# A block inversion done in place, beside a scan: fewer VectorE steps, an input copied in two parts, other PSUM banks

## The chip, the cores and the metric

The kernel runs on one core of a Trainium2 chip. The metric is device time in microseconds (us), median over runs. A core has TensorE (PE, with its weight loads shown apart as PEld), VectorE (DVE), ScalarE (ACT), GpSimd (POOL) and SyncE (SP, which issues DMAs); each takes its instructions in order. All data is float32; products that need full precision are made of three products of split operands (a high and a low part).

## The reference, cut to what matters

The model is a two-layer trunk: a spatial-gating layer, a gated ConvFFN, an RWKV-7 layer, a second ConvFFN, and a final norm, for 512 tokens of width 1024. The change lies in the RWKV-7 layer, 16 heads of width 64:

```python
kk = heads(k * k_k)
kk = kk * lax.rsqrt(jnp.maximum(jnp.sum(kk * kk, -1, keepdims=True), 1e-24))
k = k * (1 + (a - 1) * k_a)
...
y = wkv7_scan(r_h, decay, k_h, v_h, -kk, kk * a_h)

def step(state, inp):
    r_t, w_t, k_t, v_t, a_t, b_t = inp
    sa = jnp.einsum('bhvk,bhk->bhv', state, a_t)
    state = (state * w_t[:, :, None, :]
             + sa[..., None] * b_t[:, :, None, :]
             + v_t[..., None] * k_t[:, :, None, :])
    y_t = jnp.einsum('bhvk,bhk->bhv', state, r_t)
    return state, y_t
```

The kernel does this scan in chunks of 64 tokens. Within a chunk the recurrence is a triangular system, so every chunk of every head needs the inverse of a 64x64 unit triangular matrix: 8 chunks x 16 heads.

## The kernel before, in words

Tokens lie along the free axis, features along the 128 partitions: a tile is 128 features by 512 tokens, and two heads make a "pair" of 128 features. There are 8 pairs in two groups g of four. `rwkv_main` runs these generators:

- `pairs()`, per pair p: `decay` (decays and the norm of kk), `operands`, `products`. In `decay` the sum of squares of kk per head is four products of `sq` with `blk2` (two columns, one per head, L920); DVE turns the 8 columns into reciprocals (L922, L923), and PE spreads them (L928). In `products`, chunk products land in the PSUM banks "aux" (one head) and "us" (the other) (L970), are masked by DVE (L974), and ACT copies the triangular part into `ti[g]` (L975); a second set (L984) uses the same banks.
- `invert(g)`: the inverse of the 32 matrices (4 pairs x 8 chunks) per head half of group g, as 32x32 diagonal blocks on DVE and off-diagonal blocks on PE. The blocks are copied to `x` (L1035 DVE for g = 1, L1037 ACT for g = 0), transposed to `li` (L1040), and `tt` is set to the identity by POOL (L1031, L1032). A loop over j = 0 to 30 multiplies a column with a row of `li` into `pr` (L1050) and adds it to `tt` (L1051). Two transposes make `z` and `y` (L1040). Then come PE's off-diagonal products (L1069, L1072) into "aux" banks, with ACT's copies out (L1082, L1084) and of the diagonal blocks (L1077).
- `scan(g)`: the chunk recurrence of a group, a chain of small products (L1275, L1279, L1288, L1295, L1300) with DVE, ACT and POOL steps between them (L1278, L1289, L1290, L1299, L1284, L1303), and `finish`.
- `fill`: projections, gates and the output projection, whose long products keep PE busy beside the rest (L325 to L327, in `mm3`).

Every bank name has two buffers. `weave` puts the generators together: at each `yield` of the main one it takes so many steps of a side generator and of `fill`, with rates written out by hand (`RATES`). A planner then orders each engine's instructions by its own costs, so the order on an engine can differ from that of the program. The first inversion runs beside the last pairs; the second starts when the first makes its off-diagonal products, and its loop runs on beside `scan(0)`.

Of the kernel before, what the change touches and what calls it, by code (L numbers as in the profile page):

```python
# [12 lines left out]
F32 = mybir.dt.float32  # L13
F32R = mybir.dt.float32r
AF = mybir.ActivationFunctionType
ALU = mybir.AluOpType
# [4 lines left out]
P = 128  # L21
D = 1024
KT = 8
T = 512
NF = 22
C = 64
# [118 lines left out]
class Emit:  # L145
# [622 lines left out]
    def rwkv_main(self, r, ctx, gain):  # L768
        nc, tc, A = self.nc, self.tc, self.A
        V, S, G = nc.vector, nc.scalar, nc.gpsimd  # L770
# [5 lines left out]
        ip = r.ip  # L776
        ep = ctx.enter_context(tc.tile_pool(name="pairs", bufs=1))

        def tile_(shape, tag, bufs):
            return ep.tile(shape, F32, tag=tag, bufs=bufs, name=self.uid(tag))  # L780

        def tmp(tag, bufs, w=W2):
            return tile_([P, w], tag, bufs)

        def c3(t):
            return t.rearrange("p (c t) -> p c t", t=C)
# [9 lines left out]
        def second_factors(p):  # L796

            w32 = self.l2w.pop()
            l2[:] = [ep.tile([P, 2 * P], F32R, tag=f"l2{i}", bufs=1, name=self.uid("l2")) for i in range(3)]
            for j in range(2):  # L800
                w = w32[:, 512 * j:512 * j + 2 * P]
                S.copy(l2[j], w)
                V.tensor_tensor(l2[2][H[j]], w[H[j]], l2[j][H[j]].bitcast(F32), ALU.subtract)
            if p + 2 < KT:
                self.load_l2(p + 2)
# [82 lines left out]
        def scratch(tag):  # L888
            return self.gp.tile([P, T], F32, tag=tag, bufs=2 if tag == "sq" else 1, name=self.uid(tag))

        def decay(p, u):

            k, w = ks[p], slice(p % 2 * P, (p % 2 + 1) * P)
            accs = [self.acc("e") for _ in range(2)]
            for j in range(2):
                nc.tensor.matmul(accs[j], l2[j][:, w], r.lr[j], start=True, stop=False)
            for j in range(2):
                nc.tensor.matmul(accs[j], l2[2][H[j], w], r.lr[j][H[j]], start=False, stop=True)
            if p % 2 == 1 and p + 1 < KT:
                second_factors(p + 1)  # L900
            th, u.ta = scratch("sq"), tmp("ta", 2, T)
            for j, x in enumerate((th, u.ta)):
                S.activation(x, accs[j], AF.Tanh, scale=0.5, bias=dq(j, p))
            u.kn = tmp("kn", 2, T)
            S.activation(u.kn, k, AF.Copy, scale=dq(2, p))
            V.tensor_scalar(th, th, 1.0, None, ALU.add)
            yield
            V.tensor_tensor_scan(th, self.c("smask", T), th, 0.0, ALU.mult, ALU.add)
            sq = scratch("sq")
            S.activation(sq, u.kn, AF.Square)  # L910
            u.gt = tile_([P, NCH, C + 1], "gt", 1)
            G.memset(u.gt[:, :, 0:1], 1.0)
            S.activation(u.gt[:, :, 1:], c3(th), AF.Exp, scale=C1)
            S.activation(gc[:, p], c3(th)[:, :, C - 1], AF.Exp, scale=C1)
            u.ei = scratch("rb")
            S.activation(u.ei, th, AF.Exp, scale=-C1)

            q = self.acc("e")
            for b in range(4):
                nc.tensor.matmul(q[:, 2 * b:2 * b + 2], sq[:, b * P:(b + 1) * P], self.c("blk2", 2), start=True, stop=True)  # L920
            n2 = tile_([P, 8], "n2", 2)
            V.tensor_scalar(n2, q[:, 0:8], 1e-24, None, ALU.max)  # L922
            V.reciprocal(n2, n2)  # L923
            yield
            u.q = self.acc("e")
            for b in range(4):
                for hd in range(2):
                    nc.tensor.matmul(u.q[H[hd], b * P:(b + 1) * P], n2[:, 2 * b + hd:2 * b + hd + 1].to_broadcast([P, C]),  # L928
                                     self.c("ident", P), start=True, stop=True)
            yield  # L930
# [87 lines left out]
        def invert(g):  # L1018

            tg = ti[g].rearrange("p i c t -> p (i c) t")
            Q = [(slice(64 * hd + 32 * b, 64 * hd + 32 * b + 32), slice(32 * b, 32 * b + 32))
                 for hd in range(2) for b in range(2)]

            def blocks(tag):
                return ip.tile([P, 32, 32], F32, tag=tag, bufs=2, name=self.uid(tag))

            x, li, tt = blocks("ix"), blocks("li"), blocks("tt")
            pr = ip.tile([P, 272], F32, tag="pr", bufs=1, name=self.uid("pr"))  # L1030
            G.memset(tt, 0.0)  # L1031
            G.memset(tt.rearrange("p s t -> p (s t)")[:, 0:1024:33], 1.0)  # L1032
            for n, (rows, cols) in enumerate(Q):
                if g == 1:
                    V.tensor_copy(x[rows], tg[rows, :, cols])  # L1035
                else:
                    S.copy(x[rows], tg[rows, :, cols])  # L1037
            def turn(out, src):
                for bs in [slice(n, n + 8) for n in range(0, 32, 8)] if g == 1 else [slice(0, 32)]:
                    V.transpose(out[:, bs], src[:, bs])  # L1040

            turn(li.rearrange("p s t -> p t s"), x.rearrange("p u t -> p t u"))
            for _ in range(WAIT):
                yield
            for j in range(31):
                ni, nj = 31 - j, j + 1
                a = li[:, j, j + 1:32].unsqueeze(1).to_broadcast([P, nj, ni])
                b = tt[:, 0:nj, j].unsqueeze(2).to_broadcast([P, nj, ni])
                q = pr[:, 0:ni * nj].rearrange("p (c i) -> p c i", i=ni)
                V.tensor_tensor(q, a, b, ALU.mult)  # L1050
                V.tensor_tensor(tt[:, 0:nj, j + 1:32], tt[:, 0:nj, j + 1:32], q, ALU.add)  # L1051
                if j % 2 == 1:
                    yield

            z, y = blocks("ix"), blocks("li")
            turn(z.rearrange("p u t -> p t u"), tt)
            turn(y.rearrange("p u t -> p t u"), tt.rearrange("p s t -> p t s"))
            yield
            off, own = blocks("tt"), iter(Q)
            for i in range(2):  # L1060
                for hf in range(2):
                    ps = self.acc("aux").rearrange("p (u t) -> p u t", t=32)
                    us = slice(16 * hf, 16 * hf + 16)
                    for u in range(16):
                        for hd in range(2):
                            b0, b1 = Q[2 * hd][0], Q[2 * hd + 1][0]
                            n = 16 * hf + u
                            if i == 0:
                                nc.tensor.matmul(ps[b1, u, :], tg[b0, n, 32:64], z[b0, n, :], start=True, stop=True,  # L1069
                                                 tile_position=(b0.start, b1.start))  # L1070
                            else:
                                nc.tensor.matmul(ps[b0, u, :], off[b1, n, :], y[b1, n, :], start=True, stop=True,  # L1072
                                                 tile_position=(b1.start, b0.start))
                        if u % 8 == 7:
                            if i == 0:
                                rows, cols = next(own)
                                S.copy(tg[rows, :, cols], y[rows])  # L1077
                            yield
                    for hd in range(2):
                        b0, b1 = Q[2 * hd][0], Q[2 * hd + 1][0]  # L1080
                        if i == 0:
                            S.copy(off[b1, us], ps[b1])  # L1082
                        else:
                            S.copy(tg[b0, us, 32:64], ps[b0])  # L1084
# [287 lines left out]
        def until(gen, end):  # L1372
            for _ in gen:
                yield
                if end():
                    return


        fill = itertools.chain(projections(), gates(), project())
        gw, ga = {}, {}  # L1380
        main = pairs()
        self.weave(until(main, lambda: 3 in done), None, fill, *RATES[0], ktiles=STEPS[0])
        inv = invert(0)
        for _ in take(inv, FIRST0):
            pass
        self.weave(until(main, lambda: KT - 2 in done), inv, fill, *RATES[1], ktiles=STEPS[1])
        load(0, 0)
        self.weave(main, inv, fill, *RATES[5], ktiles=STEPS[1])
        ahead = invert(1)
        for _ in inv:  # L1390
            next(fill)
            self.step(ahead, (mybir.EngineType.PE,))
# [83 lines left out]
```

## Time and profile before

| | |
|---|---|
| median of 3 runs | 1255.08 us (1254.97 to 1259.6) |
| profiled execution, its own time | 1255.64 us |
| its span, first to last instruction | 1253.5 us |
| PE busy | 1235.4 us (99%) |
| PEld, DVE, ACT, POOL busy | 80%, 68%, 50%, 7% |
| mean granted PE clock | 0.997 |
| RWKV pairs and inversions, scans | about 570 to 730 us, 728 to 856 us |

Times below are of the profiled execution, counted from its span's start. A row of a stretch gives, after its length, busy time and instruction count of each engine, the granted PE clock as a share of full speed, the DMA engines' busy share, and GB/s. A row of a group ends in busy time, mean ns of one, and idle time just before. In a row of the timeline the bracket tells how long the engine stood idle before, and who ended that.

### The profile page before, as it was taken

To read this page: it belongs to the slowest core of one execution; us is meant where nothing else is said; L and a number is where in the kernel's file an instruction comes from. 1 tells how busy PE (TensorE), PEld (TensorE's weight loads), DVE (VectorE), ACT (ScalarE), POOL (GpSimd) and SP (SyncE) were. 2 spreads that over 40 slices of the span, in tenths; PEclk is the share of its full clock that TensorE was granted. 3 is DMA by queue.
4 is the path that set the end of the run, shared out by engine and by line. 5 is a ranking of instruction groups with operands and counts; after the bars stand their busy time and mean duration, and the time that the engine had idled before them with its cause. 6 is when DMAs were issued, how large, how long until landed. Compare 5 with 4: busy or idle time off the path is not lost.

```text
span 1253.5 us, 19402 instructions
## 1 busy us (share of the span) xinstructions
PE 1235.4 (99%) x7535; PEld 1002.0 (80%) x7535; DVE 857.8 (68%) x1416; ACT 628.2 (50%) x1081; POOL 83.4 (7%) x110
## 2 busy tenths in 40 slices
PE   8999999999999999999999999899999999999997
PEld 6878888888888888877777777677888888888886
DVE  5566568888886454775789898675677777772323
ACT  6544455555554333475676657433544445442322
POOL 1100200000000010000000023222100000000000
PEclk9999999999999999999999999999999999999999
DMA  7332457777656776326878797644322333233332
GB/s 269 96 106 81 134 175 244 243 250 244 202 166 205 222 219 183 108 86 189 219 199 227 220 281 215 215 152 135 101 94 92 101 101 96 91 95 97 106 93 80
DMA packets 125132, 201.65 MB, mean 161 GB/s; under 512 B 39856, under 2 KB 63152, under 8 KB 125040
## 3 DMA queue, kind: packets, MB, share of 16 engines
q10 hardware_dynamic: 38976, 112.87, 29.6%
q1 hardware_dynamic: 86064, 87.54, 22.6%
q8 instruction: 59, 0.97, 0.3%
q14 instruction: 33, 0.27, 0.1%
HBM read 152.93 MB, written 47.45 MB: 160 GB/s over the span
## 4 chain that ended last, share of the span: by engine, by line
PE 90%; DVE 5%; DMA 2%; ACT 1%; issue 1%; POOL 0%; SPq 0%; POOLq 0%; DVEq 0%; ACTq 0%
PE mm L325 9%; PE mm L326 9%; PE mm L327 9%; PE aux L325 6%; PE aux L327 6%; PE aux L326 6%; PE e L325 6%; PE e L326 6%; PE us L325 6%; PE e L327 6%; PE us L327 6%; PE us L326 6%; PE aux L970 1%; DVE tt L1051 1%; DVE pr L1050 1%; PE aux L984 1%
## 5 line engine op out<-in xcount | busy, mean ns | idle before, releaser
L237 ACT CAST w<-w 128x512 fp32r<-128x512 f32 x340 | 205.9, 611 | 350.5 <-PE aux L327 89.1
L238 DVE TENSOR_TENSOR w<-w,w 128x512 fp32r<-128x512 f32 x340 | 231.1, 682 | 181.6 <-ACT w L237 181.2
L325 PE MATMUL mm<-mxh,w 128*128 128x512 f32 x408 | 166.7, 409 | 0.0
L326 PE MATMUL mm<-mxl,w 128*128 128x512 f32 x408 | 160.9, 394 | 0.9 <-DVE mxl L1188 0.9
L327 PE MATMUL mm<-mxh,w 128*128 128x512 f32 x408 | 160.3, 393 | 0.0
L325 PEld LDWEIGHTS mm<-mxh,w 128*128 128x128 f32 x408 | 76.8, 188 | 19.6 <-issue 3.3
L326 PEld LDWEIGHTS mm<-mxl,w 128*128 128x128 f32 x408 | 76.8, 188 | 16.5 <-issue 1.3
L327 PEld LDWEIGHTS mm<-mxh,w 128*128 128x128 f32 x408 | 76.7, 188 | 16.6 <-issue 0.7
L575 ACT ACTIVATE cv<-z,par 128x512 f32<-128x512 f32 x88 | 71.7, 816 | 32.5 <-DVE z L573 27.6
L325 PE MATMUL aux<-mxh,w 128*128 128x512 f32 x216 | 84.5, 391 | 0.0
L325 PE MATMUL us<-mxh,w 128*128 128x512 f32 x216 | 84.5, 391 | 0.0
L327 PE MATMUL aux<-mxh,w 128*128 128x512 f32 x216 | 84.2, 390 | 0.0
L326 PE MATMUL aux<-mxl,w 128*128 128x512 f32 x216 | 84.1, 389 | 0.0
L326 PE MATMUL us<-mxl,w 128*128 128x512 f32 x216 | 84.1, 389 | 0.0
L327 PE MATMUL us<-mxh,w 128*128 128x512 f32 x216 | 84.1, 389 | 0.0
L354 POOL TENSOR_TENSOR ss<-ss,sq 128x512 f32<-128x512 f32 x24 | 31.8, 1325 | 760.4 <-ACT sq L352 760.4
L325 PE MATMUL e<-mxh,w 128*128 128x512 f32 x208 | 81.4, 391 | 0.0
L326 PE MATMUL e<-mxl,w 128*128 128x512 f32 x208 | 81.1, 390 | 0.0
L327 PE MATMUL e<-mxh,w 128*128 128x512 f32 x208 | 81.0, 389 | 0.0
L576 DVE SCALAR_TENSOR_TENSOR cv<-z,par,cv 128x512 f32<-128x512 f32 x88 | 66.0, 751 | 19.5 <-ACT cv L575 19.5
L577 DVE SCALAR_TENSOR_TENSOR cv<-z,par,cv 128x512 f32<-128x512 f32 x88 | 66.0, 752 | 2.9
L325 PEld LDWEIGHTS aux<-mxh,w 128*128 128x128 f32 x216 | 40.5, 188 | 9.0 <-issue 0.5
(1091 smaller groups left out, 2565.6 us busy)
## 6 DMA issues: line engine op xcount, KB each, us to landing
w<-in_wup ACTq DMA_DIRECT2D x88, 512.0 KB, 3.7
w<-in_wdn ACTq DMA_DIRECT2D x32, 512.0 KB, 3.6
st<-std SPq DMA_DIRECT2D x15, 640.0 KB, 6.4
w<-wkd ACTq DMA_DIRECT2D x16, 512.0 KB, 4.6
w<-wvd ACTq DMA_DIRECT2D x16, 512.0 KB, 5.2
w<-wod ACTq DMA_DIRECT2D x16, 512.0 KB, 4.1
w<-in_wdn ACTq DMA_DIRECT2D x16, 384.0 KB, 3.6
w<-in_wsu ACTq DMA_DIRECT2D x8, 512.0 KB, 3.9
```

Of the source, the lines that this page charges most:

```text
L237: nc.scalar.copy(hi[r, :n], src)
L238: (lo_eng or nc.vector).tensor_tensor(lo[r, :n], src, hi[r, :n].bitcast(F32), ALU.subtract)
L325: mm(acc, wh, xh, start=first, stop=False)
L326: mm(acc, wh, xl, start=False, stop=False)
L327: mm(acc, wl, xh, start=False, stop=last)
L354: nc.gpsimd.tensor_tensor(self.ss, self.ss, self.sq, ALU.add)
L575: nc.scalar.activation(c, z[:, 2:], AF.Identity, scale=cw(2, i), bias=self.p("conv_b", l * 44 + i))
L576: nc.vector.scalar_tensor_tensor(c, z[:, 1:T + 1], cw(1, i), c, ALU.mult, ALU.add)
L577: nc.vector.scalar_tensor_tensor(c, z[:, 0:T], cw(0, i), c, ALU.mult, ALU.add)
L970: nc.tensor.matmul(qs[hd][:, c - ch.start, :], bk[H[hd], c, C * hd:C * hd + P], ar[H[hd], c, :], start=True, stop=True)
L984: nc.tensor.matmul(qs[hd][:, c, :], bk[H[hd], c, C * hd:C * hd + P], dg[H[hd], c, :], start=True, stop=True)
L1050: V.tensor_tensor(q, a, b, ALU.mult)
```

## The change

In `decay`, the sum of squares is multiplied with `bones` (128 columns, one half per head) in place of `blk2`, and DVE reads every 64th column.

In `invert`:

- The loop works in place: `tt` is the transposed input itself, its diagonal set to one by DVE; POOL sets nothing. Step 0 is left out, and each other step treats j columns in place of j + 1. Steps 1 and 30 are a single DVE instruction that multiplies and adds. Tile "tt" goes, and the off-diagonal result has a tile "off" with one buffer.
- For g = 1 the input is copied in two parts: blocks 0 to 23 (pairs 4 to 6) by ACT, in a first step that is called before the last pair's weave; blocks 24 to 31 by DVE in the next step.
- For g = 0 the off-diagonal products go to "e" banks, and a step of `fill` is put between the transposes to `z` and `y`.

```diff
-                nc.tensor.matmul(q[:, 2 * b:2 * b + 2], sq[:, b * P:(b + 1) * P], self.c("blk2", 2), start=True, stop=True)
+                nc.tensor.matmul(q[:, b * P:(b + 1) * P], sq[:, b * P:(b + 1) * P], self.c("bones", P), start=True, stop=True)
...
-            V.tensor_scalar(n2, q[:, 0:8], 1e-24, None, ALU.max)
+            V.tensor_scalar(n2, q[:, 0:T:C], 1e-24, None, ALU.max)
...
-            x, li, tt = blocks("ix"), blocks("li"), blocks("tt")
+            x = blocks("ix")
             pr = ip.tile([P, 272], F32, tag="pr", bufs=1, name=self.uid("pr"))
-            G.memset(tt, 0.0)
-            G.memset(tt.rearrange("p s t -> p (s t)")[:, 0:1024:33], 1.0)
-            for n, (rows, cols) in enumerate(Q):
-                if g == 1:
-                    V.tensor_copy(x[rows], tg[rows, :, cols])
-                else:
-                    S.copy(x[rows], tg[rows, :, cols])
+            cut = 24 * g
+            for us in (slice(0, cut), slice(cut, 32))[1 - g:]:
+                for rows, cols in Q:
+                    if us.start and g == 1:
+                        V.tensor_copy(x[rows, us], tg[rows, us, cols])
+                    else:
+                        S.copy(x[rows, us], tg[rows, us, cols])
+                if g == 1 and us.start == 0:
+                    yield
...
-            turn(li.rearrange("p s t -> p t s"), x.rearrange("p u t -> p t u"))
+            tt = blocks("li")
+            turn(tt.rearrange("p s t -> p t s"), x.rearrange("p u t -> p t u"))
+            V.memset(tt.rearrange("p s t -> p (s t)")[:, 0:1024:33], 1.0)
...
-            for j in range(31):
-                ni, nj = 31 - j, j + 1
-                a = li[:, j, j + 1:32].unsqueeze(1).to_broadcast([P, nj, ni])
-                b = tt[:, 0:nj, j].unsqueeze(2).to_broadcast([P, nj, ni])
-                q = pr[:, 0:ni * nj].rearrange("p (c i) -> p c i", i=ni)
-                V.tensor_tensor(q, a, b, ALU.mult)
-                V.tensor_tensor(tt[:, 0:nj, j + 1:32], tt[:, 0:nj, j + 1:32], q, ALU.add)
+            for j in range(1, 31):
+                ni = 31 - j
+                to = tt[:, 0:j, j + 1:32]
+                if j == 1:
+                    V.scalar_tensor_tensor(to[:, 0], tt[:, 1, 2:32], tt[:, 0, 1:2], to[:, 0], ALU.mult, ALU.add)
+                elif ni == 1:
+                    V.scalar_tensor_tensor(to[:, :, 0], tt[:, 0:j, j], tt[:, j, 31:32], to[:, :, 0], ALU.mult, ALU.add)
+                else:
+                    a = tt[:, j, j + 1:32].unsqueeze(1).to_broadcast([P, j, ni])
+                    b = tt[:, 0:j, j].unsqueeze(2).to_broadcast([P, j, ni])
+                    q = pr[:, 0:ni * j].rearrange("p (c i) -> p c i", i=ni)
+                    V.tensor_tensor(q, a, b, ALU.mult)
+                    V.tensor_tensor(to, to, q, ALU.add)
...
             turn(z.rearrange("p u t -> p t u"), tt)
+            if g == 0:
+                next(fill)
             turn(y.rearrange("p u t -> p t u"), tt.rearrange("p s t -> p t s"))
             yield
-            off, own = blocks("tt"), iter(Q)
+            off, own = blocks("off"), iter(Q)
...
-                    ps = self.acc("aux").rearrange("p (u t) -> p u t", t=32)
+                    ps = self.acc("aux" if g == 1 else "e").rearrange("p (u t) -> p u t", t=32)
...
         load(0, 0)
+        ahead = invert(1)
+        next(ahead)
         self.weave(main, inv, fill, *RATES[5], ktiles=STEPS[1])
-        ahead = invert(1)
         for _ in inv:
             next(fill)
             self.step(ahead, (mybir.EngineType.PE,))
```

More of the change, by code (lines that the diff above doesn't have):

```diff
@@ L1026, in blocks @@
             def blocks(tag):
-                return ip.tile([P, 32, 32], F32, tag=tag, bufs=2, name=self.uid(tag))
-            x, li, tt = blocks("ix"), blocks("li"), blocks("tt")
+                return ip.tile([P, 32, 32], F32, tag=tag, bufs=1 if tag == "off" else 2, name=self.uid(tag))
+            x = blocks("ix")
             pr = ip.tile([P, 272], F32, tag="pr", bufs=1, name=self.uid("pr"))
-            G.memset(tt, 0.0)
-            G.memset(tt.rearrange("p s t -> p (s t)")[:, 0:1024:33], 1.0)
-            for n, (rows, cols) in enumerate(Q):
-                if g == 1:
-                    V.tensor_copy(x[rows], tg[rows, :, cols])
-                else:
-                    S.copy(x[rows], tg[rows, :, cols])
+            cut = 24 * g
[7 more added lines that the diff above has]
+                    yield
             def turn(out, src):
```

## The prediction, made before the changed kernel was run

> **What bounds the kernel now.** I read the page first, then the busy time by stretches around the two block inversions, then the waits of TensorE (PE), and last the timeline.
>
> ```profile
> span 1253.5 us, 19402 instructions
> PE 1235.4 (99%) x7535; PEld 1002.0 (80%) x7535; DVE 857.8 (68%) x1416; ACT 628.2 (50%) x1081; POOL 83.4 (7%) x110
> PE 90%; DVE 5%; DMA 2%; ACT 1%; issue 1%; POOL 0%; SPq 0%; POOLq 0%; DVEq 0%; ACTq 0%
> ```
>
> PE is busy for 99% of the span, and the chain that ended last lies on it for 90%. The change leaves the amount of PE's work alone but for one item, so it can gain only where PE stands idle or runs at a lower clock. The chain's 5% on VectorE (DVE) is to be looked for. Stretches (us; busy PE, PEld, DVE, ACT, POOL; granted clock; DMA share; GB/s):
>
> ```profile
> 700.00:720.00 20.00, 19.47 (x269) 15.30 (x268) 15.06 (x29) 12.25 (x21) 1.12 (x2) 1.00 0.66 183
> 720.00:740.00 20.00, 18.98 (x282) 14.81 (x280) 18.88 (x49) 11.89 (x25) 2.69 (x5) 1.00 0.87 267
> 740.00:760.00 20.00, 19.97 (x273) 14.72 (x271) 19.44 (x47) 10.24 (x23) 6.10 (x7) 1.00 0.91 276
> 760.00:780.00 20.00, 18.82 (x399) 14.77 (x398) 15.73 (x39) 16.73 (x29) 5.59 (x7) 0.91 0.71 221
> 780.00:800.00 20.00, 18.25 (x333) 13.90 (x333) 15.03 (x31) 12.32 (x26) 6.49 (x6) 1.00 0.67 218
> 800.00:820.00 20.00, 18.32 (x248) 13.24 (x244) 12.80 (x26) 7.78 (x17) 5.63 (x7) 1.00 0.54 166
> 820.00:840.00 20.00, 20.00 (x253) 15.52 (x252) 15.24 (x34) 5.61 (x14) 4.41 (x5) 1.00 0.61 189
> 840.00:860.00 20.00, 19.09 (x173) 15.18 (x172) 11.58 (x29) 4.33 (x11) 3.27 (x2) 1.00 0.41 133
> ...
> 735.00:768.00 33.00, 31.79 (x456) 23.49 (x456) 31.91 (x78) 19.55 (x42) 11.12 (x13) 1.00 0.91 270
> ...
> 706.00:708.00 2.00, 1.47 (x36) 0.96 (x34) 2.00 (x2) 0.00 (x0) 0.00 (x0) 1.00 0.97 293
> ...
> 730.00:732.00 2.00, 0.98 (x18) 0.61 (x17) 1.93 (x5) 1.36 (x3) 0.00 (x0) 1.00 1.03 318
> ...
> 766.00:768.00 2.00, 0.96 (x28) 0.90 (x29) 1.91 (x4) 1.98 (x3) 1.88 (x2) 1.00 0.45 70
> 768.00:770.00 2.00, 2.00 (x48) 1.37 (x46) 2.00 (x4) 1.96 (x4) 0.19 (x1) 0.77 0.94 376
> 770.00:772.00 2.00, 2.00 (x21) 1.88 (x22) 0.44 (x2) 1.23 (x3) 0.00 (x0) 0.50 0.51 139
> 772.00:774.00 2.00, 2.00 (x34) 1.43 (x33) 1.77 (x6) 1.94 (x3) 0.00 (x0) 0.87 0.07 27
> ```
>
> From 700 to 860 us PE idles 0.53+1.02+0.03+1.18+1.75+1.68+0+0.91 = 7.1 us. The low clock from 768 to 774 takes another 2x(0.23+0.50+0.13) = 1.72 us. These 8.8 us are the ceiling. DVE is the fullest engine from 735 to 768 (31.91 of 33 us), where the second inversion runs beside the first scan. Three of PE's holes are ended by DVE:
>
> ```profile
> PE us L1275 <- DVE vu L1299: 1.5, 2, 1.1
> PE us L1288 <- DVE wt L1278: 1.0, 1, 1.0
> PE aux L1069 <- DVE ix L1040: 0.5, 1, 0.5
> ```
>
> They are the holes at 707 (0.53), 731 (1.02) and 766 us (1.04). The low clock follows on the third.
>
> **The banks.** In the timeline (start, duration, engine, line; in brackets the idle time before and who ended it):
>
> ```profile
> 709.22 1.05 ACT L1077 COPY ti<-li 32x1024 f32<-32x1024 f32 x1 [4.84 <-DVE li L1040]
> ...
> 712.17 1.17 ACT L1082 COPY tt<-aux 32x512 f32<-32x512 f32 x2
> ...
> 713.39 0.18 PEld L970 LDWEIGHTS aux<-ar,bk 64*128 64x128 f32 x1
> ...
> 714.58 0.69 DVE L974 TENSOR_TENSOR lq<-aux,cst 128x512 f32<-128x512 f32 x1 [3.00 <-PE aux L970]
> ...
> 716.65 2.78 DVE L1035 COPY ix<-ti 32x1024 f32<-32x1024 f32 x4 [0.78 <-ACT ti L975]
> 719.47 2.26 DVE L1040 STREAM_TRANSPOSE li<-ix 128x256 f32<-128x256 f32 x4
> 721.83 0.19 DVE L1050 TENSOR_TENSOR pr<-li,tt 128x31 f32<-128x31 f32 x1
> ```
>
> The first inversion's off-diagonal products and the last pair's products share two "aux" banks. The last pair's second half (L970 at 713.39) starts as L1082's two copies out of "aux" end, at 713.34; DVE waits 3.00 us for it, then 0.78 us for ACT. With the products in "e" this order of events goes. The pairs' own use of "e" is over by then, and the scan's first use comes after L1084's copies. DVE can then start the second inversion up to 3.78 us sooner. On PE nothing is added. The next limit is ACT, whose L1077 copies wait for DVE's transposes; I take the 3.78 as an upper end and zero as the lower.
>
> **The extra fill step.** One step of projection work is put between the two transposes of the first inversion. It is moved, not added, and covers the 0.53 us at 707. If the fill ran out one step sooner it would cost as much later; the 20.00 of 20 us at 820 to 840 say that it does not run short there. Value -0.53, bounds -0.53 and 0. The weight loads that such a step issues on ACT's queue come one step sooner with it, and none of PE's waits is on a DMA.
>
> **The second input in two parts.** ACT copies 24 of the 32 blocks early, DVE the last 8.
>
> ```profile
> L1037 ACT COPY ix<-ti 32x1024 f32<-32x1024 f32 x4 | 4.2, 1044 | 0.0
> ...
> L1050 DVE TENSOR_TENSOR pr<-li,tt 128x31 f32<-128x31 f32 x4 | 0.8, 204 | 0.2
> L1050 DVE TENSOR_TENSOR pr<-li,tt 128x60 f32<-128x60 f32 x4 | 0.9, 218 | 0.1
> L1050 DVE TENSOR_TENSOR pr<-li,tt 128x256 f32<-128x256 f32 x2 | 0.8, 421 | 0.0
> ...
> L1032 POOL MEMSET tt<- 128x32 f32 x1 | 0.2, 163 | 0.1
> ```
>
> DVE's four copies took 2.78 us. At a quarter of the size and a fixed part they take some 0.9, so 1.9 us goes from DVE where it is full (bounds 1.1 and 2.1). ACT gets four copies of 768 elements, 4 x 1.04 x 0.75 and a little, 3.3 us. The gap of 4.84 us that ACT has before 709.22 holds them; their source, pairs 4 to 6, is written by then. Behind them on ACT wait the last pair's L975 copies, L854, which frees a product bank, and the loads of projection weights that ACT issues; PE waits for the first two through DVE and the bank. If the gap is not where they fall, PE can wait up to 3.3 us for ACT. I charge 0.3 us.
>
> **The inversion in place.** Step 0 goes (two instructions of 31 elements, 2 x 0.20 = 0.41 us); steps 1 and 30 become one instruction each (0.42 less). The 56 others shrink by 31-j elements: 2 x 434 elements, at (421-204)/225 = 0.96 ns each, 0.83 us. The diagonal's memset comes to DVE from POOL, 0.16. Together 1.5 us per inversion. POOL's large memset goes from an idle engine and is worth nothing. In the first inversion the 1.5 us bring the transpose at 705 forward, inside the covered 0.53.
>
> So DVE is up to 3.78 + 1.9 + 1.5 + 1.5 = 8.7 us ahead when the scan starts. This is not 8.7 us of time, since PE is nearly full beside it. It is what takes DVE's backlog from the holes at 731 (-1.02) and 766.
>
> ```profile
> 763.16 2.00 DVE L1040 STREAM_TRANSPOSE ix<-tt 128x256 f32<-128x256 f32 x4
> ...
> 767.04 0.69 PE L1275 MATMUL us<-vu,st 128*64 128x64 f32 x16 [1.12 <-DVE vu L1299]
> ```
>
> At 766 the scan's L1299 stands behind a burst of the last transposes. The burst stays, at another place of the scan; I count -1.0, bounds -1.04 and 0. With the hole I let the low clock go, -1.72, bounds -1.72 and 0.
>
> **The wider sums.** Eight times four products of 2 columns become 128 columns wide. A group of the old kind, one of the width to come (L865, same shapes), and the start of what follows each:
>
> ```profile
> 647.55 0.95 PE L920 MATMUL e<-cst,sq 128*128 128x2 f32 x8
> ...
> 648.36 0.48 PE L327 MATMUL mm<-mxh,w 128*128 128x512 f32 x1
> ...
> 701.75 1.05 PE L865 MATMUL mm<-cst,v 128*128 128x128 f32 x8
> ...
> 702.56 0.47 PE L325 MATMUL mm<-mxh,w 128*128 128x512 f32 x1
> ```
>
> Both hold PE for 0.81 us from first start to the next start, so the width is free there. Only the end is 0.10 us later, for a DVE step with other work around it. Value 0; bounds 0 and 8 x 0.10 = +0.8. [...]
>
> **Sum.** -0.53 - 1.02 - 1.0 - 1.72 + 0.3 + 0 = -4.0 us. The profiled execution took 1255.64 us (2.14 around its span), 0.56 above the median 1255.08. So 1251.6 for it, and 1251.1 for the median.
>
> **Rivals.**
>
> A clock drop stays (1252.8). The three holes close, but the drop follows on the kind of work and not on the hole: the stretch has many small products, and the hole at 731, as long, was followed by clock 1.00. Then -4.0 + 1.72 = -2.3. For it: that second hole. Against it: the drop is the only one between 700 and 860, and begins right behind the hole. [...]
>
> The holes move (1254.6). PE waits as long under other lines, because the scan is a chain of PE, DVE and ACT steps and only the 0.53 goes. For it: the 1.75 and 1.68 us between 780 and 820, where DVE is not full. Against it: 735 to 768 is full on DVE.
>
> More comes back (1247.1). The scan, started with DVE ahead, also loses most of the later holes: 8.0 of the 8.8 us. For it: 8.7 us of DVE lead. Against it: after 770 little of the inversion is left on DVE.
>
> Slower (1259.6). The early ACT copies do not fall in the 4.84 us gap but ahead of the last pair's evacuations. PE waits for 3.3 us, the clock drops once more (1.72), and of the gains the 0.5 at 707 remains: +4.5. It decides once ACT's copies are issued less than 3.3 us before ACT's next wanted copy.
>
> **How the numbers follow.** Forecast 0.38 (own range 1248.5 to 1252.5); clock drop stays 0.20; holes move 0.15; more 0.18; slower 0.09. From 1246 to 1256.5 all are in but the slower case and a part of the better one, some 0.14. A measurement of this kernel can tell about 0.5%, 6.3 us, from no change: below 1248.8 lie the case "more" and 0.07 of the forecast, 0.25; above 1261.4 a third of the slower case, 0.03; between, 0.72.
>
> **What would show it.** DVE's wait for L970 of 3.00 us gone; the second inversion's first step some 5 us before 721.83; DVE clearly under 31.91 in 33 us beside the first scan; PE full at 707, 731 and 766, and the clock 1.00 throughout; L920's groups at 0.81 us. Wrong it would be if PE's idle time between 700 and 860 stayed near 7 us, or if ACT became the one that PE waits for near 705 to 715.

## The result and the profile after

| | before | after |
|---|---|---|
| median (range) | 1255.26 us (1253.43 to 1259.6) | 1251.24 us (1251.11 to 1252.09) |
| ratio of after to before | | 0.9969, 95% interval 0.9957 to 0.998 |
| profiled execution, its own time | 1255.64 us | 1251.21 us |

The kernel got faster by 4.0 us, 0.3%, which lies inside the bound of 0.5%. The page of the kernel after, its first lines:

```profile
span 1249.1 us, 19398 instructions
PE 1230.1 (98%) x7535; PEld 998.0 (80%) x7535; DVE 854.0 (68%) x1410; ACT 632.6 (51%) x1085; POOL 82.8 (7%) x106
```

As many PE instructions as before (7535) are busy for 5.3 us less (1235.4 to 1230.1), while the span is 4.4 us shorter. So PE idles 0.9 us more than before, and the time came from inside what is shown as busy. Four stretches that hold all of the difference (30 to 560 us is alike), first of the kernel before, then after, with shorter stretches below them (columns as in the prediction; the last of the four reaches past the end of both spans):

```profile
0.00:30.00 30.00, 26.85 (x113) 19.84 (x113) 17.28 (x23) 17.77 (x30) 2.27 (x15) 1.00 0.79 274
560.00:700.00 140.00, 139.85 (x1021) 107.79 (x1021) 112.04 (x213) 94.36 (x178) 1.39 (x9) 1.00 0.77 214
700.00:870.00 170.00, 162.90 (x2250) 125.72 (x2249) 128.66 (x286) 85.03 (x168) 37.58 (x47) 0.99 0.66 203
870.00:1260.00 390.00, 375.84 (x1730) 313.04 (x1728) 233.99 (x344) 163.66 (x261) 16.30 (x14) 0.99 0.30 94
```

```profile
0.00:30.00 30.00, 28.21 (x117) 20.98 (x118) 17.54 (x24) 18.61 (x31) 3.05 (x16) 1.00 0.79 276
560.00:700.00 140.00, 138.10 (x1019) 106.85 (x1018) 114.57 (x225) 94.20 (x178) 1.40 (x9) 1.00 0.79 216
700.00:870.00 170.00, 162.39 (x2266) 125.29 (x2264) 124.10 (x271) 91.06 (x176) 39.49 (x46) 1.00 0.65 204
870.00:1260.00 390.00, 371.42 (x1710) 309.37 (x1708) 231.02 (x340) 160.70 (x257) 14.40 (x12) 0.99 0.30 92
...
735.00:768.00 33.00, 31.22 (x456) 23.00 (x456) 31.00 (x74) 19.39 (x40) 10.79 (x12) 1.00 0.94 288
...
706.00:708.00 2.00, 2.00 (x56) 1.59 (x56) 0.46 (x1) 1.94 (x5) 0.00 (x0) 1.00 0.24 86
...
730.00:732.00 2.00, 1.99 (x25) 1.84 (x26) 1.94 (x5) 0.46 (x2) 0.00 (x0) 1.00 0.93 337
...
766.00:768.00 2.00, 2.00 (x37) 1.30 (x35) 1.78 (x4) 1.95 (x4) 1.77 (x2) 1.00 0.98 392
768.00:770.00 2.00, 2.00 (x56) 1.79 (x54) 1.26 (x3) 1.95 (x3) 0.00 (x0) 1.00 0.34 124
```

Idle time of PE: 3.15 to 1.79 us in the first 30 us, which the change doesn't touch; 0.15 to 1.90 from 560 to 700; 7.1 to 7.6 from 700 to 870. The three holes of before (707, 731, 766) are full and the low clock behind 766 is gone, but holes of the same sum stand elsewhere. The waits of PE from 700 to 860 us, then the end of the largest hole (1.35 us, from 724.74 on), then a wait of DVE from 690 to 770 us:

```profile
PE us L1300 <- DVE wt L1290: 2.1, 3, 0.9
PE mm L325 <- DVE rt L882: 1.5, 2, 1.3
```

```profile
726.09 0.50 PE L325 MATMUL mm<-mxh,w 128*128 128x512 f32 x1 [1.35 <-DVE rt L882]
```

```profile
DVE lq L974 <- PE us L970: 3.2, 1, 3.2
```

The largest hole is new and ends with L882, which runs on DVE at 725.37, between steps of the second inversion's loop. So DVE's inversion holds PE up here too, at another line.

DVE's wait for L970 did not go. The timeline of the kernel after:

```profile
708.35 0.83 ACT L1037 COPY ix<-ti 32x768 f32<-32x768 f32 x1
...
713.44 1.67 ACT L1037 COPY ix<-ti 32x768 f32<-32x768 f32 x2
715.13 0.41 ACT L975 COPY ti<-lq 64x256 f32<-64x256 f32 x1
...
713.53 0.69 DVE L974 TENSOR_TENSOR lq<-aux,cst 128x512 f32<-128x512 f32 x1 [3.16 <-PE us L970]
...
715.57 0.58 DVE L1035 COPY ix<-ti 32x256 f32<-32x256 f32 x2 [0.75 <-ACT ti L975]
717.06 0.59 DVE L1035 COPY ix<-ti 32x256 f32<-32x256 f32 x2 [0.92 <-ACT ti L975]
...
719.89 0.21 DVE L1053 SCALAR_TENSOR_TENSOR li<-li 128x30 f32<-128x30 f32 x1
```

ACT's early copies stand between 708 and 715, ahead of the last pair's L975, and not in the gap before 709 where the prediction put them. The second inversion's first step comes at 719.89, 1.94 us sooner than before, and not 5.

What did become shorter inside PE's busy time shows in the last pair's products. A product of L970 stands as 64*128 in its row, where one of L325 stands as 128*128: it is on 64 of the 128 partitions, one half for each head of the pair. Before (first fence), the 16 products of one set stood 8 and 8, the "us" half at 704.12 and the "aux" half at 708.02; after, the halves alternate from 706.29 to the next instruction at 707.38:

```profile
704.12 1.16 PE L970 MATMUL us<-ar,bk 64*128 64x128 f32 x8
...
708.02 1.16 PE L970 MATMUL aux<-ar,bk 64*128 64x128 f32 x8
```

```profile
706.29 0.37 PE L970 MATMUL aux<-ar,bk 64*128 64x128 f32 x1
706.29 0.37 PE L970 MATMUL us<-ar,bk 64*128 64x128 f32 x1
...
707.18 0.27 PE L970 MATMUL us<-ar,bk 64*128 64x128 f32 x1
707.38 0.79 PE L1081 MATMUL e<-ix,ti 32*32 32x32 f32 x38
```

Alternating, 16 take 1.09 us. Eight of one half alone, from first start to the next product's, take 1.08, so the eight of the other half add 0.01 us where the halves alternate. The last pair's second set took 1.47 before and 1.09 after. Together the last pair's L970 went from 3.63 to 2.18 us, 1.45 us, and none of it was idle time in the profile.

### The profile page after: what moved, and what is told of

Its sections match the earlier page's. It is cut to its first block, busy times and chain, and to the rows that moved or that the text cites. A ratio compares the mean times of both kernels' runs of the same rounds, so it can differ in the third digit from the quotient of the medians.

```text
span 1249.1 us, 19398 instructions
## 1 busy us (share of the span) xinstructions
PE 1230.1 (98%) x7535; PEld 998.0 (80%) x7535; DVE 854.0 (68%) x1410; ACT 632.6 (51%) x1085; POOL 82.8 (7%) x106
## 4 chain that ended last, share of the span: by engine, by line
PE 39%; DVE 6%; ACT 2%; issue 2%; POOL 1%; DVEq 0%; POOLq 0%; ACTq 0%
PE mm L325 4%; PE mm L326 4%; PE mm L327 4%; PE e L326 3%; PE e L327 3%; PE e L325 3%; PE aux L325 2%; PE aux L326 2%; PE aux L327 2%; PE us L326 2%; PE us L327 2%; PE us L325 2%; DVE pr L1060 1%; DVE li L1061 1%; PE us L1300 1%
## 5 line engine op out<-in xcount | busy, mean ns | idle before, releaser
L325 PE MATMUL mm<-mxh,w 128*128 128x512 f32 x408 | 167.9, 412 | 1.5 <-DVE rt L882 1.5
L325 PEld LDWEIGHTS mm<-mxh,w 128*128 128x128 f32 x408 | 76.6, 188 | 22.7 <-issue 4.4
L325 PE MATMUL aux<-mxh,w 128*128 128x512 f32 x216 | 84.5, 391 | 0.0
L325 PE MATMUL us<-mxh,w 128*128 128x512 f32 x216 | 84.5, 391 | 0.0
L325 PE MATMUL e<-mxh,w 128*128 128x512 f32 x208 | 81.4, 391 | 0.0
L325 PEld LDWEIGHTS aux<-mxh,w 128*128 128x128 f32 x216 | 40.5, 188 | 9.1 <-issue 0.5
```

Of the source, the lines that this page charges most:

```text
L325: mm(acc, wh, xh, start=first, stop=False)
```

## The experiments

Each is told by its median, its ratio to the kernel before with the 95% interval, and the mean granted clock over its runs.

### One part put back at a time

The sums: `blk2` and 2 columns in the kernel after.

> The changed kernel with the narrow sums (2 columns) put back. Lead theory (the gain is VectorE's lead over the first scan, the width is free on TensorE): 1251.2 us, within 0.6. Order theory (the gain hangs on where the planner's order leaves TensorE waiting, any edit can move that): anything from 1250 to 1255, with other holes. If the wide sums themselves were the gain: near 1255.

The banks:

```diff
-                    ps = self.acc("aux" if g == 1 else "e").rearrange("p (u t) -> p u t", t=32)
+                    ps = self.acc("aux").rearrange("p (u t) -> p u t", t=32)
```

> The changed kernel with the first inversion's products back in the aux banks. Lead theory: the last pair waits for a bank again, VectorE starts the second inversion some 1 us later (in the changed kernel's trace the wait did not vanish, it only moved, so the banks' share of the lead is about 1 us and not 3.8); time 1251.2 to 1252.5. Order theory: 1250 to 1255, with no relation to the start of the second inversion.

The copy: one part, DVE's for g = 1, and `ahead = invert(1)` behind the weave again.

> The changed kernel with the second inversion's input copied in one part by VectorE, after the last pair. Lead theory: VectorE copies for 2.8 us instead of 2.1, but ScalarE is free of four copies of 0.83 us that stood ahead of the last pair's own copies in the changed kernel's trace; the second inversion starts within 1 us of where it does now; 1250.8 to 1252.2. Order theory: 1250 to 1255.

The loop: identity by POOL, step 0, steps 1 and 30 in two instructions each, in both inversions.

> The changed kernel with the old loop of the inversion (identity set by GpSimd, 31 steps of two instructions). Lead theory: VectorE has 1.5 us more to do in each inversion, the hole and the clock drop behind the second one's last transposes come back: 1253 to 1255. Order theory: 1250 to 1255, with or without the clock drop.

| kernel after with | median (range), us | ratio to before | mean clock |
|---|---|---|---|
| narrow sums | 1251.69 (1251.01 to 1252.21) | 0.9970 [0.9956, 0.9983] | 0.9986 |
| "aux" banks | 1251.63 (1250.69 to 1253.19) | 0.9968 [0.9956, 0.9979] | 0.9980 |
| one-part copy | 1251.06 (1250.61 to 1252.29) | 0.9962 [0.9947, 0.9977] | 0.9982 |
| old loop | 1254.59 (1252.45 to 1255.45) | 0.9991 [0.9981, 1.0002] | 0.9968 |

Sums, banks and copy can each be taken out and nothing is lost that these runs can tell. Without the loop 3.35 of 4.0 us go. The lead theory, in which banks and copy make 5.7 of the 8.7 us of DVE's lead, is not borne out. It looked as if the loop carried it all, and the runs of before pointed to a second thing: 1253 us at a mean clock of 0.998 or 0.999, 1258 and more at 0.993 to 0.994.

### The loop alone, and the clock

The loop alone is the kernel before with the loop of the diff.

> The kernel before with the in-place inversion alone, in both inversions (no step 0, steps 1 and 30 in one instruction, the diagonal's memset on VectorE); one-part copy, old banks, narrow sums, no extra fill step. Loop theory (the in-place loop carries the gain alone: 3.4 of 4 us went when it was put back): 1251.3 to 1252.0, some 3.5 us under the kernel before, with no drop of the granted clock near 768 in the profile and a mean clock of 0.998 or 0.999 in most runs. Lead theory of the prediction (the loop is 3.0 of the 8.7 us by which VectorE gets ahead, and the hole at 766 needs all of it): 1253.7 to 1254.5, a third of the gain, and the hole behind L1299's burst still there.

Dummy products in the hole at 766:

```diff
+                if (g, c) == (0, 5):
+                    with tc.issue_after(self.last(mybir.EngineType.PE)):
+                        idle()
                 lead = batch(lambda i, hd, n: nc.tensor.matmul(us[H[hd], 0, i, :], both(i, hd, 0), vu[:, hd, i, :],
```

> The kernel before with two dummy products more (L1103, 128 x 256 columns into a spare half of a bank, 0.38 us each by the row of L1103) ahead of the scan's products that waited 1.12 us at 766; they fill the hole with work that serves nothing. Clock theory (about half of the gain is the granted clock: the drop at 768 to 774, 1.72 us, follows the hole at 766, and comes and goes from run to run): 1253.2 to 1253.8, and a narrower spread than the kernel before, since the runs with a mean clock of 0.993 to 0.997 go. Rival (the clock drops for the many small products of the stretch, not for the hole, or drops elsewhere in the runs): 1255 to 1256 with the same spread as before, the two dummy products costing up to 0.8 us.

The old loop in one inversion of the kernel after (`if g == 0:` or `if g == 1:` around it):

> The kernel after with the old loop (identity from POOL, step 0, two instructions in steps 1 and 30) in the first inversion only. Theory that the second inversion carries it, since it alone runs beside a full VectorE and the first scan: 1251.2 to 1251.6, no change from after. Rival (the first inversion sets the hole at 700 to 707 and the start of the rest): 1253 to 1254.6, most of the 3.4 us that the old loop cost in both, with a hole of 1 to 2.6 us near 700 ahead of L1076.

> The kernel after with the old loop in the second inversion only. Theory that the second inversion carries it: 1253.5 to 1254.6, with the clock at 0.996 or 0.997 in most runs (drops near 770 to 790 come back). Rival (the first inversion carries it): 1251.2 to 1252.0. If both are near 1253, the loop's worth is shared, and the drops come from either.

| kernel | median (range), us | ratio to before | mean clock |
|---|---|---|---|
| before + loop | 1258.83 (1255.77 to 1264.78) | 1.0033 [1.0017, 1.0048] | 0.9938 |
| before + dummies at 766 | 1254.83 (1253.3 to 1256.29) | 0.9992 [0.9980, 1.0004] | 0.9973 |
| after, old loop in the first | 1252.16 (1250.21 to 1254.01) | 0.9973 [0.9962, 0.9984] | 0.9972 |
| after, old loop in the second | 1251.93 (1251.2 to 1253.39) | 0.9972 [0.9961, 0.9982] | 0.9980 |

The loop alone made the kernel slower; both theories had missed. Either inversion can keep the old loop at 0.7 to 0.9 us, against 3.35 for both: neither carries the gain, and the loop's worth is no sum over the two. The dummies gave 0.7 of the 2 us that the clock theory asked for, not told from zero by its interval; the runs below 0.996 went, those at 0.996 and 0.997 stayed. Stretches of the loop alone:

```profile
704.00:706.00 2.00, 1.40 (x39) 1.17 (x38) 2.00 (x2) 0.07 (x1) 0.00 (x0) 1.00 0.57 133
706.00:708.00 2.00, 2.00 (x45) 1.84 (x44) 1.94 (x3) 0.82 (x1) 0.00 (x0) 0.96 0.95 290
...
718.00:720.00 2.00, 2.00 (x19) 1.89 (x19) 1.95 (x5) 0.33 (x2) 0.00 (x0) 1.00 0.50 117
720.00:722.00 2.00, 2.00 (x18) 2.00 (x16) 1.82 (x8) 0.55 (x1) 0.00 (x0) 0.87 0.01 4
...
728.00:730.00 2.00, 2.00 (x38) 1.43 (x37) 0.51 (x1) 0.66 (x2) 0.00 (x0) 0.92 0.46 95
```

and its timeline there, above the first and last row of the same products in the kernel before:

```profile
717.87 2.00 PE L984 MATMUL us<-dg,bk 64*128 64x64 f32 x16
...
719.97 2.31 PE L984 MATMUL aux<-dg,bk 64*128 64x64 f32 x16
```

```profile
717.51 0.99 PE L984 MATMUL us<-dg,bk 64*128 64x64 f32 x7
...
719.90 0.38 PE L984 MATMUL aux<-dg,bk 64*128 64x64 f32 x2
```

Here the two halves run one after the other, 16 and 16, in 4.3 us to the next product (part of it at half clock) where before they alternated in part and took 2.7 (in the kernel after they alternate from first to last and take 1.93). PE shows as full, and the clock still falls, at 721.48 (a slice of 2 us at 0.87 is at half clock for 2 x 0.13 / 0.5 = 0.52 us), until 728.32, and is 0.50 from 722 to 728. So this low clock came with no idle time of PE in the profile: PE is busy for 2.00 of 2 us in each slice from 706 to 722, and the products from 717.87 on are, but for two, those of the two halves (64x64), 16 and 16. An earlier low stretch of this trace, from 707.84 to 711.24, came behind a hole of 0.60 us.

### The fill step

The fill step was the one part not taken out so far. Its edit is the two lines `if g == 0:` / `next(fill)` between the transposes, out of the kernel after, into the kernel before with the loop, and into the kernel before alone.

> The kernel after without the extra fill step between the two transposes of the first inversion. So far the loop put alone on the kernel before made it slower (ratio 1.0033, mean granted clocks down to 0.989), while the kernel after with the sums, the banks or the copy put back stayed at 1251 to 1251.7. The one part not yet taken out is the fill step. Fill theory (the in-place loop pays only with the fill step, because without it the hole at 705 comes with two drops of the clock between 707 and 729): 1254.5 to 1257, mean clocks mostly 0.996 or less. Rival (the loop pays with any of the other parts, and the fill step is worth the 0.5 us of its hole at most): 1251.2 to 1252.

> The kernel before with the in-place loop and the extra fill step; one-part copy, old banks, narrow sums. Fill theory (the two together are the change): 1251 to 1252.5, the clock 1.00 between 700 and 730 in the profile. Rival (the new banks or the copy are what makes the loop pay): 1255 to 1259, as with the loop alone.

> The kernel before with the extra fill step alone. Prediction's term (the step covers the 0.53 us at 707, and nothing else changes): 1254.5 to 1255. Theory that the fill step keeps the clock up as well: 1253 to 1254. Rival (each part alone upsets the order of the queues as the loop alone did): 1256 or more.

| median, ratio, mean clock | old loop | loop in place |
|---|---|---|
| before, no fill step | 1255.3, 1, 0.9968 | 1258.83, 1.0033 [1.0017, 1.0048], 0.9938 |
| before, fill step | 1256.7, 1.0017 [1.0002, 1.0033], 0.9929 | 1252.1, 0.9977 [0.9966, 0.9988], 0.9972 |
| the rest of the change too, no fill step | not run | 1255.5, 1.0003 [0.9994, 1.0011], 0.9967 |
| the rest of the change too, fill step | 1254.59, 0.9991 [0.9981, 1.0002], 0.9968 | 1251.24, 0.9969 [0.9957, 0.9980], 0.9985 |

Each of the two alone makes the kernel slower, and together they give 3.2 of the 4.0 us. The fill theory held in both of its tests, and the prediction's term for the fill step alone (1254.5 to 1255) did not.

The runs of the fill step alone go from 1251.13 us (mean clock 0.999) to 1262.87 (0.987), so its time goes with the clock. Over the 230 runs with a clock on record, a line through time against mean clock, one slope for all and a level for each kernel, gives 0.99 us (error 0.04) for each 0.001 of clock lost. At a clock of 0.999 the levels are 1253.4 before, 1254.1 loop alone, 1251.3 fill alone, 1250.8 both, 1250.9 after, 1252.2 after with the old loop, 1253.3 after without the fill step, each to 0.3 to 0.7. By that estimate 2.5 of the 4 us are other than clock, and some 1.7 are the clock (0.9985 against 0.9968).

The part other than clock goes with the fill step: 2.1, 3.3 and 2.4 us in the three pairs of kernels that differ in that step alone, against -0.7, 0.5 and 1.3 in the three that differ in the loop alone. The loop's part is mostly the clock, and its sign depends on the fill step: the mean clock falls from 0.9968 to 0.9938 without the step, and rises from 0.9929 to 0.9972 and from 0.9968 to 0.9985 with it. This split is an estimate from runs; the kernel of the next section tests the clock's part.

The low stretches have one length, or twice that. Rows of the kernel after without the fill step, at the start and end of two of them:

```profile
702.00:703.00 1.00, 0.27 (x10) 0.27 (x12) 1.00 (x2) 0.23 (x1) 0.00 (x0) 0.71 0.66 211
709.00:710.00 1.00, 1.00 (x6) 0.58 (x4) 0.00 (x0) 0.96 (x3) 0.00 (x0) 0.88 0.00 0
801.00:802.00 1.00, 0.73 (x16) 0.77 (x16) 0.16 (x1) 0.98 (x3) 0.93 (x2) 0.70 0.82 332
804.00:805.00 1.00, 1.00 (x5) 0.36 (x3) 0.00 (x0) 0.00 (x0) 0.00 (x0) 0.59 0.80 300
```

By the arithmetic above they last from 702.42 to 709.24 (6.82 us) and from 801.40 to 804.82 (3.42), and begin 98.98 us apart, 29 x 3.413. The kernel before's lasted 2 x 1.72 = 3.44, that of the loop alone 6.84. In the loop alone the drops of 707.84 and 721.48 begin 13.64 us apart, 4 x 3.41. An estimate from these lengths and distances is that the clock changes at ticks some 3.41 us apart. Drops came behind holes of 0.60 us (the loop alone) and 1.12 us (the kernel before).

Where the holes fall against such ticks could be why the same program drops in some runs and not in others. That is a guess; the simplest form of it, that idle time between two ticks decides, can be held against two traces. In the kernel after the clock falls once at the end, behind PE's last product, where that costs nothing, and so shows a tick:

```profile
1245.00:1246.00 1.00, 0.00 (x0) 0.00 (x0) 0.00 (x1) 0.00 (x0) 0.00 (x0) 0.57 1.04 337
```

That is at 1245.14 (the clock is 0.50 from 1246 on). Counted back in steps of 3.413, by the estimate, two ticks lie at 722.9 and 726.3 with the whole hole of 1.35 us between them, and no drop followed. In the loop alone the 3.41 us that end at the drop of 707.84 hold 0.60 us of idle time. So idle time between two ticks does not decide alone. What does stays open.

### The clock tested by itself

```diff
+                        if (g, i, hf, u) == (1, 0, 0, 7):
+                            with tc.issue_after(self.last(mybir.EngineType.PE)):
+                                idle()
```

> The kernel with the fill step alone (1256.7 us, mean clocks 0.987 to 0.999, and in its profile a low clock from 768.96 to 775.6 behind 1.0 us of idle time in three pieces between 766 and 768), and nothing changed but two dummy products more (L1108, 128 x 256 columns into a spare half of a bank) right ahead of the second of those three pieces; every other instruction stands in TensorE's queue where it stood. They add some 0.9 us of work, in time that was idle. Clock theory (what made the fill step alone slow are the drops of the clock behind those pieces; by clock, its runs come to 1251.7 where it stays up): 1253 to 1254.5, mean clocks mostly 0.996 or more. Rival (the drops come from the kind of work or from elsewhere in the 1250 us): 1256.5 to 1257.5 with mean clocks around 0.993, as without them.

1254.29 us (1251.85 to 1259.53), ratio 0.9992 [0.9976, 1.0009], mean clock 0.9962. First the stretches with the fill step alone, then with the two dummies more:

```profile
766.00:768.00 2.00, 1.10 (x4) 0.67 (x4) 1.97 (x5) 1.96 (x3) 0.26 (x1) 1.00 0.85 323
768.00:770.00 2.00, 1.99 (x23) 1.25 (x23) 1.75 (x3) 1.98 (x4) 1.47 (x2) 0.73 0.62 237
```

```profile
766.00:768.00 2.00, 1.84 (x8) 1.18 (x8) 1.97 (x5) 1.96 (x3) 0.31 (x1) 1.00 0.88 341
768.00:770.00 2.00, 1.97 (x37) 1.29 (x35) 1.75 (x3) 1.98 (x4) 1.42 (x2) 1.00 0.58 216
```

Two products that compute nothing made the kernel with the fill step faster, from 1256.7 by 2.4 us, and the mean clock rose from 0.9929 to 0.9962. The intervals of the two ratios, [1.0002, 1.0033] and [0.9976, 1.0009], overlap a little, and the two kernels were timed on different chips, each beside the kernel before, so the size is rough. Three of its twelve runs are still at 0.993 and 1258 us or more, so other places drop as well. The place that the clock theory named is right, and is not the only one.

No kernel beats the one after by more than its interval. The nearest, the kernel after with the one-part copy (0.9962), leaves out a part that brought nothing.

## Why the prediction was right in its number and wrong in its steps

The number came out within 0.2 us of the median (1251.1 against 1251.24). The working behind it did not, so the closeness of the number is luck.

- **The base step failed: "it can gain only where PE stands idle or runs at a lower clock".** PE idled 0.9 us more and the kernel was still 4.4 us shorter in the profiled executions. Of the 5.3 us of busy time that went, 1.72 are the clock, which the prediction had; 1.45 are the last pair's L970 with its halves side by side, and 0.77 its L984 (2.70 to 1.93); the remaining 1.4 are spread over small amounts and not traced. So the busy share did not tell what PE could still save: the last pair's first 2 x 8 products of L970 were shown as busy for 2.2 us before, and 1.09 did after.
- **Banks, up to 3.78 us of lead: wrong.** The wait behind L970 is 3.16 us now, and taking the banks back changed nothing (1251.63). PE, busy for 19.88 of the 20 us from 700 to 720, comes to L970's second set at 712.33 in its turn: the wait is for L970's place in PE's queue, not for the bank.
- **Fill step, -0.53: wrong in mechanism and size.** The hole at 707 is full in the kernel after, but the step does not fill it: with the step alone it is 0.68 us, with step and loop 0.91:

```profile
706.97 0.69 PE L1071 MATMUL aux<-ix,ti 32*32 32x32 f32 x32 [0.68 <-DVE ix L1040]
```

```profile
705.42 0.69 PE L1077 MATMUL aux<-ix,ti 32*32 32x32 f32 x32 [0.91 <-DVE ix L1038]
```

  Alone the step cost 1.4 us, by its clock; with the loop and the rest it is worth 4.3 (1255.5 to 1251.24), and at equal clock some 2 to 3 by the estimate above.
- **Two-part copy:** DVE's L1035 went from 2.74 to 1.14 us (1.6; 1.9 predicted). ACT's L1037 grew by 3.30 (3.3 predicted), but not in the gap. DVE waits 1.67 us for L975 behind it. The charge of 0.3 isn't seen, nor is a gain.
- **Loop, 1.5 us of DVE per inversion: right.** The group of before and after:

```profile
L1051 DVE TENSOR_TENSOR tt<-tt,pr 128x31 f32<-128x31 f32 (+15 forms) x62 | 22.0, 355 | 1.2
```

```profile
L1060 DVE TENSOR_TENSOR pr<-li 128x58 f32<-128x58 f32 (+13 forms) x56 | 20.4, 364 | 1.2
L1061 DVE TENSOR_TENSOR li<-li,pr 128x58 f32<-128x58 f32 (+13 forms) x56 | 19.7, 352 | 1.2
```

  With L1050 as long as L1051, and the single steps (0.98) and the memset (0.17) added, 44.0 became 41.2: 1.37 each. What this does to the time was not to be had from it: -4.6 us with the fill step, +3.5 without.
- **Holes at 731 and 766, -1.0 each:** both closed, and others came (1.35 us from 724.7 on, and 0.6 to 0.7 ahead of 730, 757 and 759). From 735 to 768 DVE is as full as before (31.00 against 31.91 of 33). What the prediction named as proof against itself, idle time near 7 us, came true.
- **Clock, -1.72: right** in the profile (1.00 until PE's last product), and in the runs (0.9968 to 0.9985). The reason was too narrow: the loop alone has a drop with PE full, so the rival that laid it to the kind of work had a share of the truth.
- **Wider sums, 0:** from first start to the next product 0.81 us in two of the eight groups and 0.91 to 1.09 in six, 7.45 us in all against 6.75. That is +0.70, near the upper bound of 0.8. One such group and its next product, after:

```profile
661.43 1.16 PE L920 MATMUL e<-cst,sq 128*128 128x128 f32 x8 [0.65 <-ACT sq L910]
662.52 0.32 PE L984 MATMUL aux<-dg,bk 64*128 64x64 f32 x1
```

  A cost that the prediction put at nothing came with them: from 560 to 700 PE idles 1.90 us in place of 0.15, 0.9 of it ahead of L920:

```profile
PE e L920 <- ACT sq L910: 0.9, 2, 0.6
```

  With the narrow sums back that idle time is 0.10, but from 700 to 870 it is 8.61 in place of 7.61, and the median was 0.45 higher, not lower. So nothing of the cost reaches the end that these runs can tell.
- **Rivals.** "The holes move" was right of the idle time, yet its 1254.6 us assumed that idle time was all. "Slower" had its mechanism come true, ACT's early copies ahead of L975, and PE did not wait for it (full from 706 to 710).
- **Luck.** 1.36 us of the profiled 4.4 are a shorter idle time in the first 30 us, where nothing was changed. It differs from one execution to another: in the other traces PE is busy for 27.05 to 28.26 us of these 30.

What stays open: why loop and fill step need each other. The planner orders PE's queue anew after each edit. In the kernel before with either one alone, the halves of L970 and L984 stand apart in places. In the kernel after without one of them they do not (L970 1.09 and 1.09, L984 1.93), but the hole ahead of the first off-diagonal product is 1.18 us without the fill step and 2.6 with the old loop, against none in the kernel after. That hole alone is not the reason: with the narrow sums put back it is 0.8 us, at no loss that the runs can tell. How these make up the levels and the drops of the clock was not shown.

## What to carry to other kernels

Before a gain is summed from parts, ask whether the parts share a planned order: then take out each part, and also each pair that fails alone, since here two edits that lost 3.5 and 1.4 us gave 3.2 together. Compare kernels at equal mean clock as well as by their medians: here that showed one edit shortening the work and the other mostly moving the clock. Treat a PE that is shown as 99% busy as unproven: look for products on 64 of the 128 partitions that stand alone where those of the other 64 could alternate with them (here 2.2 us against 1.09), and for the granted clock in every run, not in the profiled one only. Here 3.44 us at half clock came behind a hole of 1.12 us, and two dummy products ahead of another drop were worth some 2.4 us, so a filler of no use can pay.

## What the runs showed of the hardware

- The low stretches read from the traces lasted 3.40, 3.42, 3.44, 6.82 and 6.84 us, at a granted clock of 0.50; by an estimate, half of 3.4, each 3.4 us of them costs 1.7 us where PE is busy. They came behind holes of 0.60 us and 1.12 us, not behind one of 1.35 (between two ticks, by the estimate above), and once with PE shown as busy throughout the 14 us before (706 to 721.48), among products of the two halves that did not alternate.
- How often the clock fell varied from run to run of one program: mean clock 0.987 to 0.999, and with it 1262.87 to 1251.13 us, 11.7 us, for the fill step alone.
- Products of L970 (64*128) on alternating halves start in pairs, two at 706.29 in the kernel after: 16 take 1.09 us, and 8 of one half alone took 1.08 in the kernel before.
